# Dilated attention with upper and lower heads issued in turn, gates behind the attention, the memory's key slabs at the end

## The chip, the cores and the metric

The kernel runs on one core of a Trainium2 chip. The metric is the device time of one execution in microseconds (us). The engines are TensorE (PE; its weight loads are listed as PEld), VectorE (DVE), ScalarE (ACT), GpSimd (POOL) and SyncE (SP), which issues the large DMAs. Each engine works through its own list of instructions in a fixed order. An instruction whose input is late holds up everything behind it on its engine.

## The reference

A stream of 256 tokens with 1024 features goes through two blocks of layers. Only one part is touched here, the mixer of the second block and the memory attention that follows it:

```python
h = rmsnorm_2(x, mix_norm[l])
z = h @ w_in[l]                       # 2 x 512 for the gate, 3 x 512 for q, k, v
z_sgu = jax.nn.gelu(z[..., :2 * D_SGU], approximate=False)
...
y_a = chunked_spatial_gating(z_sgu, sgu_ln_g[l], sgu_ln_b[l], sgu_w_s[l], sgu_b_s[l])
y_b = dilated_mixture_attention(q, k, v).reshape(b, s, D_ATT)
y = jnp.concatenate([rmsnorm_2(y_a, out_norm_a[l]), rmsnorm_2(y_b, out_norm_b[l])], axis=-1)
x = x + y @ w_out[l]
h = rmsnorm_2(x, cross_norm[l])
m = rmsnorm_2(mem, mem_norm[l])
x = x + memory_cross_attention(h, m, cross_wq[l], cross_wk[l], cross_wv[l], cross_wo[l])
```

The dilated attention has 8 heads of 64 features. The kernel computes it as one softmax attention whose mask carries the logarithm of how many of the three dilated patterns contain a key. The gate normalises one half of `z_sgu` in groups of 64, mixes it along the tokens with a causal 128x128 matrix per group, and multiplies the result with the other half.

## The kernel before, in words

The activation `x` stays on the chip with features on the partitions. Weights come in slabs of 1 MB. SP loads a slab into one of two `raw` buffers (line 277), ACT rounds each half to `whi` (line 293), DVE computes the rest `wlo` (line 295). Five half slabs can be alive at once, and a slab is prepared two slabs ahead of its use (`W_AHEAD = 2`). A `raw` buffer is free again when the second `wlo` of its slab is done. A product with a slab is three matmuls per tile (lines 320 to 322).

Matmul results go to PSUM. There are eight banks: two called `mm`, two `tr`, four `acc`. Each name is a ring: a new tile takes the bank of the oldest tile of that name, once that one has been read.

The order of the mixer's work is written out in the string `MIX`. Its words:

- `v`, `w`, `x`, `y` are products of the normed tokens with two slabs of `w_in` each. `v` feeds the gate's values (`gate_values`: gelu, group norm over several DVE passes, one pow on POOL). `w` and `x` give q and k, `y` gives the attention's values.
- `r0`, `r1` turn q and k by their positions and transpose them, for the first and the second 128 tokens.
- `u0`, `u1` are the other half of the gate (one slab each, gelu in `gates`).
- `00`, `01` and `10` to `13` are steps of the attention, for the first and the second 128 tokens.
- `g0`, `g1` are the gate's mixing matmuls (`gating`, line 1357) with the multiplication and the norm behind them (`normed`).
- `N` loads and norms the memory (into a `raw` buffer). `K0` to `K3` are its four slabs of keys.

Behind the string stands the output product `w_out`.

A step of the attention before handles 4 heads (first tokens) or 2 heads (second tokens, with twice the keys). All heads of a step lie in the same half of the partitions. The step adds the mask by two matmuls with the identity (line 587), computes the scores (line 591, 64 of 128 rows of the array), the softmax on DVE and ACT (lines 594 to 612), transposes the probabilities (line 401), copies them (line 619), and multiplies with the values (line 625, 64 of 128 columns). The instructions' final order on each engine is set by a scheduler that moves instructions of later words ahead where their inputs allow, as far as the rings of buffers let it.

Of the kernel before, what the change touches and what calls it, by code (L numbers as in the profile page):

```python
# [12 lines left out]
AF = mybir.ActivationFunctionType  # L13
ALU = mybir.AluOpType
AX = mybir.AxisListType

P = 128
# [7 lines left out]
SCALE = 0.125  # L25
# [21 lines left out]

EVEN = "p0 i0 N x1 W0 t0 p1 i1 h0 W1 h1 i2 m0 m1 00 x0 10 i3 W2 s0 W3 11 12 01 x2 m2 g0 13 g1 g2 m3 x3 g3"

MIX = "x N v w y r0 r1 u0 10 u1 00 K0 11 g0 01 12 g1 13 K1 K2 K3"  # L50


def weight_plan():
# [14 lines left out]
    def ffn(kind, layer):  # L68
        for c in range(11):
            feat(f"{kind}_gate", layer, c * 256, 256)  # L70
            feat(f"{kind}_up", layer, c * 256, 256)
        for c in range(11):
            plan.append((f"{kind}_down", layer, "d", c * 16, 0))
# [29 lines left out]
    ffn("ffn1", 0)  # L103
    for f in MIX.split():
        if f[0] in "vwxy":
# [132 lines left out]
class Kernel:  # L238
# [331 lines left out]
    def attention(self, pool, t, qt, kt, kblock, v, vcol, bias, nsink):  # L570

        nc = self.nc
        nk = t + 1
        per = 4 // nk
        keys = nk * P
        den = self.small([P, 8], "den")
        mneg = self.small([P, 8], "mneg")
        mx = self.small([P, 8], "mx")  # L580
        po = self.ps("acc")

        def step(g):
            sc = self.ps("mm")
            scv = sc.rearrange("p (h k) -> p h k", h=per)
            for m, bt in enumerate(bias):
                nc.tensor.matmul(sc, self.ident_r, bt, start=(m == 0), stop=False)
            for i in range(per):
                half, qb = divmod(g * per + i, 4)
                r = slice(half * 64, half * 64 + 64)  # L590
                nc.tensor.matmul(scv[:, i, :], qt[r, qb, t * P:(t + 1) * P],  # L591
                                 kt[r, kblock(qb), 0:keys], start=False, stop=(i == per - 1))
            hs = slice(g * per, (g + 1) * per)
            nc.vector.tensor_reduce(mx[:, hs], scv, axis=AX.X, op=ALU.max)
            if nsink is None:
                nc.vector.tensor_scalar(mneg[:, hs], mx[:, hs], -SCALE, None, ALU.mult)
            else:
                nc.vector.scalar_tensor_tensor(mneg[:, hs], mx[:, hs], -SCALE, nsink[:, hs],
                                               ALU.mult, ALU.min)
                es = self.small([P, per], f"es{per}")  # L600
                nc.vector.tensor_tensor(es, mneg[:, hs], nsink[:, hs], ALU.subtract)
            pr = self.t(pool, [P, per, keys], "prob", bufs=4)
            for i in range(per):
                h = g * per + i
                nc.scalar.activation(pr[:, i, :], scv[:, i, :], AF.Exp, bias=mneg[:, h:h + 1],
                                     scale=SCALE, accum_out=den[:, h:h + 1])
            if nsink is not None:
                nc.scalar.activation(es, es, AF.Exp)
                nc.vector.tensor_tensor(den[:, hs], den[:, hs], es, ALU.add)
            nc.vector.reciprocal(den[:, hs], den[:, hs])  # L610
            e = nc.gpsimd if nsink is not None and NORMP[t] == "g" else nc.vector
            e.tensor_tensor(pr, pr, den[:, hs].unsqueeze(2).to_broadcast([P, per, keys]), ALU.mult)
            tp = self.ps("tr")
            for i in range(per):
                for b in range(nk):
                    c = i * nk + b
                    self.transpose(tp[:, c * P:(c + 1) * P], pr[:, i, b * P:(b + 1) * P])
            pt = self.t(pool, [P, 4, P], "prob", bufs=4)
            nc.scalar.copy(pt, tp.rearrange("p (c n) -> p c n", c=4))
            for i in range(per):  # L620
                half, qb = divmod(g * per + i, 4)
                r = slice(half * 64, half * 64 + 64)
                h = 2 * qb + half
                for b in range(nk):
                    nc.tensor.matmul(po[r, qb * P:(qb + 1) * P], v[b][:, vcol(h):vcol(h) + 64],  # L625
                                     pt[:, i * nk + b, :], start=(b == 0), stop=(b == nk - 1))

        return [lambda g=g: step(g) for g in range(8 // per)], po.rearrange("p (b n) -> p b n", b=4)


    def setup(self):
# [632 lines left out]
    def mix(self):  # L1264
        nc, a = self.nc, self.a
        stack = ExitStack()
        mp = self.pool("mix", stack=stack)
# [34 lines left out]
        vt = [self.t(mp, [P, 512], f"vt{t}") for t in range(NT)]  # L1302
        qt, kt = self.t(mp, [P, 4, 256], "qt"), self.t(mp, [P, 4, 256], "kt")
        oa, ob = self.operand(), self.operand()

        def normed(y, gain, op, t):

            sq = self.t(self.wk, [P, 512], "sq", bufs=2)
            nc.scalar.activation(sq.rearrange("p (b n) -> p b n", b=4), y, AF.Square)
            nc.gpsimd.tensor_tensor(sq[:, :256], sq[:, :256], sq[:, 256:], ALU.add)  # L1310
            r, _ = self.inv_rms([sq[:, b * P:(b + 1) * P] for b in range(2)], 512, 1e-6, "rn")
            yn = self.t(mp, [P, 4, P], "yn", bufs=2)
            for b in range(4):
                nc.vector.scalar_tensor_tensor(yn[:, b, :], y[:, b, :], self.prm[:, gain + b:gain + b + 1],
                                               r, ALU.mult, ALU.mult)
            s = slice(t * P, (t + 1) * P)
            self.split_ps(yn, op[0][:, :, s], op[1][:, :, s])

        def dilated(t):
            v = qk[:, t].rearrange("p i (h d) -> p (i h) d", d=64)  # L1320
            x1, x2 = v[:, :, 0:8], v[:, :, 8:16]
            c = self.cos[:, t, :].unsqueeze(1).to_broadcast([P, 16, 8])
            s = self.sin[:, t, :].unsqueeze(1).to_broadcast([P, 16, 8])
            t1, t2, t3, t4 = (self.t(mp, [P, 16, 8], f"ro{i}", bufs=2) for i in range(4))
            nc.vector.tensor_tensor(t1, x1, c, ALU.mult)
            nc.vector.tensor_tensor(t2, x2, s, ALU.mult)
            nc.vector.tensor_tensor(t3, x2, c, ALU.mult)
            nc.vector.tensor_tensor(t4, x1, s, ALU.mult)
            nc.vector.tensor_tensor(x1, t1, t2, ALU.subtract)
            nc.vector.tensor_tensor(x2, t3, t4, ALU.add)  # L1330
            for i, dst in enumerate((qt, kt)):
                ps = self.ps("tr")
                for b in range(4):
                    self.transpose(ps[:, b * P:(b + 1) * P], qk[:, t, i, b * P:(b + 1) * P])
                d = dst[:, :, t * P:(t + 1) * P]
                if i == 0:
                    nc.scalar.copy(d, ps.rearrange("p (b n) -> p b n", b=4))
                else:
                    nc.vector.tensor_copy(d, ps.rearrange("p (b n) -> p b n", b=4))
            if t == 0:  # L1340
                bias = [x[:, 128:].unsqueeze(1).to_broadcast([P, 4, P]) for x in (dh, dl)]
            else:
                bias = [x.unsqueeze(1).to_broadcast([P, 2, 256]) for x in (dh, dl)]
            return self.attention(mp, t, qt, kt, lambda b: b, vt, lambda h: h * 64, bias, None)

        su = self.t(mp, [P, 4, 256], "su")

# [3 lines left out]
            nc.scalar.activation(d, d, AF.Gelu)  # L1351

        def gating(t):
            ps = self.ps("acc")
            for g in range(8):
                r = slice((g % 2) * 64, (g % 2) * 64 + 64)
                nc.tensor.matmul(ps[r, (g // 2) * P:(g // 2 + 1) * P], sv[t][:, g * 64:(g + 1) * 64],
                                 ws[:, g, :], start=True, stop=True)
            ya = self.t(mp, [P, 4, P], "ya", bufs=2)
            nc.vector.tensor_tensor(ya, ps.rearrange("p (b n) -> p b n", b=4), bst, ALU.add)  # L1360
            nc.vector.tensor_tensor(ya, ya, su[:, :, t * P:(t + 1) * P], ALU.mult)
            normed(ya, PR_ONA, oa, t)
# [3 lines left out]
        def step(t, i):  # L1366
            att[t][0][i]()
            if i + 1 == len(att[t][0]):
                normed(att[t][1], PR_ONB, ob, t)

        for f in MIX.split():
            c = int(f[1:] or 0)
            if f == "v":
                self.gemm_tok(ops, "w_in", 0, 512, gate_values)
            elif f in "wxy":
                i = "wxy".index(f)
# [182 lines left out]
```

## Time and profile before

| what | us |
|---|---|
| median of 3 runs (1245.34 to 1247.02) | 1246.55 |
| the profiled execution | 1243.83 |
| its span | 1242.1 |
| PE busy | 1211.7 |
| DVE busy | 868.8 |
| ACT busy | 676.6 |
| POOL busy | 211.2 |

The span is the stretch between the first and the last recorded instruction. A busy PE is not a PE at its peak: matmuls overlap, and 64-row or 64-column matmuls use half of the array. The mixer lies at about 850 to 980 us of the span; its attention at 903 to 953 us. What the kernel can win or lose there is read from the time that PE spends on its attention's matmuls and from the time it waits between them.

### The profile page before, as it was taken

To read this page: it belongs to the slowest core of one execution; us is meant where nothing else is said; L and a number is where in the kernel's file an instruction comes from. 1 tells how busy PE (TensorE), PEld (TensorE's weight loads), DVE (VectorE), ACT (ScalarE), POOL (GpSimd) and SP (SyncE) were. 2 spreads that over 40 slices of the span, in tenths; PEclk is the share of its full clock that TensorE was granted. 3 is DMA by queue.
4 is the path that set the end of the run, shared out by engine and by line. 5 is a ranking of instruction groups with operands and counts; after the bars stand their busy time and mean duration, and the time that the engine had idled before them with its cause. 6 is when DMAs were issued, how large, how long until landed. Compare 5 with 4: busy or idle time off the path is not lost.

```text
span 1242.1 us, 19044 instructions
## 1 busy us (share of the span) xinstructions
PE 1211.7 (98%) x7686; PEld 1072.7 (86%) x7686; DVE 868.8 (70%) x1191; ACT 676.6 (54%) x1052; POOL 211.2 (17%) x177
## 2 busy tenths in 40 slices
PE   6889999999999999999999999999999999999997
PEld 6777998888899879888888888888889999888886
DVE  8978588777665647877766867766866656777752
ACT  6543566565446755655545655545664545655542
POOL 7665021110010002101001110002201101111000
PEclk9978999999999999999999999999999999999998
DMA  6541355555553325455654545646633434555551
GB/s 208 172 158 53 139 172 194 180 201 203 180 197 110 131 68 204 170 187 186 216 191 174 196 177 198 204 174 212 209 131 103 155 118 139 190 183 201 204 200 38
DMA packets 36776, 208.86 MB, mean 168 GB/s; under 512 B 3920, under 2 KB 9808, under 8 KB 12752
## 3 DMA queue, kind: packets, MB, share of 16 engines
q1 hardware_dynamic: 35824, 205.48, 47.7%
q0 software_dynamic: 576, 1.64, 0.5%
q8 instruction: 60, 0.98, 0.3%
q10 hardware_dynamic: 288, 0.52, 0.1%
q14 instruction: 28, 0.23, 0.1%
HBM read 205.57 MB, written 2.06 MB: 167 GB/s over the span
## 4 chain that ended last, share of the span: by engine, by line
PE 92%; DVE 5%; DMA 1%; issue 1%; ACT 1%; POOL 0%; DVEq 0%; ACTq 0%
PE acc L367 26%; PE acc L366 13%; PE mm L367 13%; PE mm L366 7%; PE mm L320 4%; PE mm L322 4%; PE mm L321 4%; PE acc L322 4%; PE acc L321 4%; PE acc L320 4%; PE mm L591 1%; PE tr L401 1%; PE acc L1191 1%; DVE wlo L295 1%; PE acc L625 1%; DVE a L454 1%
## 5 line engine op out<-in xcount | busy, mean ns | idle before, releaser
L295 DVE TENSOR_TENSOR wlo<-raw,whi 128x1024 fp32r<-128x1024 f32 (+1 forms) x378 | 472.0, 1251 | 225.1 <-ACT whi L293 223.6
L293 ACT CAST whi<-raw 128x1024 fp32r<-128x1024 f32 (+1 forms) x378 | 392.4, 1043 | 280.8 <-DMA raw<-in_wts 111.2
L367 PE MATMUL acc<-h,whi 128*128 128x512 f32 x704 | 247.8, 397 | 0.0
L367 PE MATMUL mm<-a,whi 128*128 128x512 f32 x704 | 247.0, 392 | 0.0
L367 PE MATMUL acc<-a,whi 128*128 128x512 f32 x704 | 246.0, 392 | 0.0
L366 PE MATMUL acc<-h,wlo 128*128 128x256 f32 x704 | 196.9, 281 | 0.0
L366 PE MATMUL mm<-a,wlo 128*128 128x256 f32 x704 | 196.6, 281 | 0.0
L366 PE MATMUL acc<-a,wlo 128*128 128x256 f32 x704 | 196.3, 280 | 0.0
L367 PEld LDWEIGHTS acc<-h,whi 128*128 128x128 f32 x704 | 131.9, 188 | 32.0
L367 PEld LDWEIGHTS mm<-a,whi 128*128 128x128 f32 x704 | 131.5, 187 | 28.5
L367 PEld LDWEIGHTS acc<-a,whi 128*128 128x128 f32 x704 | 130.9, 187 | 28.2
L366 PEld LDWEIGHTS acc<-a,wlo 128*128 128x128 f32 x704 | 133.0, 189 | 1.0
L366 PEld LDWEIGHTS acc<-h,wlo 128*128 128x128 f32 x704 | 132.9, 189 | 0.3
L366 PEld LDWEIGHTS mm<-a,wlo 128*128 128x128 f32 x704 | 132.6, 189 | 0.2
L546 POOL TENSOR_TENSOR sg<-sg,rb 128x512 f32<-128x512 f32 x44 | 58.2, 1326 | 388.8 <-ACT sg L545 379.2
L463 POOL TENSOR_TENSOR ssq<-ssq,sq 128x512 f32<-128x512 f32 x26 | 39.7, 1528 | 416.7 <-ACT sq L461 253.2
L320 PE MATMUL mm<-a,whi 128*128 128x256 f32 x224 | 66.4, 298 | 6.7 <-ACT whi L293 6.7
L321 PE MATMUL acc<-a,whi 128*128 128x256 f32 x240 | 67.4, 284 | 0.0
L322 PE MATMUL acc<-a,wlo 128*128 128x256 f32 x240 | 67.1, 285 | 0.0
L322 PE MATMUL mm<-a,wlo 128*128 128x256 f32 x224 | 66.1, 296 | 0.8 <-DVE wlo L295 0.7
L320 PE MATMUL acc<-a,whi 128*128 128x256 f32 x240 | 66.0, 286 | 0.0
L321 PE MATMUL mm<-a,whi 128*128 128x256 f32 x224 | 65.8, 295 | 0.0
(371 smaller groups left out, 1951.5 us busy)
## 6 DMA issues: line engine op xcount, KB each, us to landing
raw<-in_wts SPq DMA_DIRECT2D x187, 1024.0 KB, 4.9
raw<-in_mem SPq DMA_DIRECT2D x4, 512.0 KB, 5.6
eb<-lag SPq DMA_DIRECT2D x4, 512.0 KB, 4.8
x<-in_x SPq DMA_DIRECT2D x4, 256.0 KB, 5.3
raw<-in_wts SPq DMA_DIRECT2D x4, 256.0 KB, 5.6
sprm<-in_prm SPq DMA_DIRECT2D x1, 512.0 KB, 9.1
ud<-s SPq DMA_DIRECT2D x1, 512.0 KB, 2.6
uu<-ud SPq DMA_DIRECT2D x8, 64.0 KB, 5.3
```

Source lines behind the costliest of these rows:

```text
L293: nc.scalar.copy(hi[:, c:c + n], src)
L295: nc.vector.tensor_tensor(lo[:, c:c + n], src, hi[:, c:c + n].bitcast(F32), ALU.subtract)
L320: mm(out, a[0], b[0], start=start, stop=False, skip_group_check=True)
L321: mm(out, a[0], b[1], start=False, stop=False, skip_group_check=True)
L322: mm(out, a[1], b[0], start=False, stop=stop, skip_group_check=True)
L366: mm(out[:, 0, :], w[1], x[:, 0], start=first, stop=False, skip_group_check=True)
L367: mm(out, w[0], x, start=False, stop=last, skip_group_check=True)
L401: self.nc.tensor.transpose(out, in_, self.ident[:k, :k])
L454: lo = nc.vector.scalar_tensor_tensor(lo, x[:, b, :], g, hi.bitcast(F32), ALU.mult, ALU.subtract).ins
L463: nc.gpsimd.tensor_tensor(ssq, ssq, q, ALU.add)
L546: nc.gpsimd.tensor_tensor(sg, sg, rb2, ALU.mult)
L591: nc.tensor.matmul(scv[:, i, :], qt[r, qb, t * P:(t + 1) * P], kt[r, kblock(qb), 0:keys], start=False, stop=(i == per - 1))
```

## The change

A new function, `attention_pairs`, takes the place of `attention` in the mixer. One of its steps handles heads of both halves of the partitions: 8 heads for the first tokens (one step, `00`), 4 heads for the second (two steps, `10` and `11`). Scores of the lower and of the upper half follow each other in turn, each into a bank of its own, and so do the products with the values. Masks, transposes, softmax instructions and copies keep their number. The scores now take two `acc` banks per step instead of one `mm` bank, and the gate's mixing takes an `mm` bank instead of an `acc` bank. The probabilities of a step have one transposed buffer (`probt`) instead of a share in a ring of four.

The order string puts the memory's norm `N` between `u0` and `u1`, the value product `v` behind the first attention steps, both gates behind the last one, and all four key slabs at the end.

```diff
-MIX = "x N v w y r0 r1 u0 10 u1 00 K0 11 g0 01 12 g1 13 K1 K2 K3"
+MIX = "x w y r0 r1 10 00 v 11 u0 N u1 g0 g1 K0 K1 K2 K3"
...
+    def attention_pairs(self, pool, t, qt, kt, v, bias):
+        nc = self.nc
+        nk = t + 1
+        per = 4 // nk
+        keys = nk * P
...
+        po = self.ps("acc")
+
+        def softmax(half, g, scv, pt):
+            hs = slice(half * 4 + g * per, half * 4 + (g + 1) * per)
+            nc.vector.tensor_reduce(mx[:, hs], scv, axis=AX.X, op=ALU.max)
+            nc.vector.tensor_scalar(mneg[:, hs], mx[:, hs], -SCALE, None, ALU.mult)
+            pr = self.t(pool, [P, per, keys], "prob", bufs=2)
+            for i in range(per):
+                h = hs.start + i
+                nc.scalar.activation(pr[:, i, :], scv[:, i, :], AF.Exp, bias=mneg[:, h:h + 1],
+                                     scale=SCALE, accum_out=den[:, h:h + 1])
+            nc.vector.reciprocal(den[:, hs], den[:, hs])
+            nc.vector.tensor_tensor(pr, pr, den[:, hs].unsqueeze(2).to_broadcast([P, per, keys]), ALU.mult)
+            tp = self.ps("tr")
...
+            nc.scalar.copy(pt, tp.rearrange("p (c n) -> p c n", c=4))
+
+        def step(g):
+            scs = [self.ps("acc") for _ in range(2)]
...
+            for i in range(per):
+                qb = g * per + i
+                for half in range(2):
+                    r = slice(half * 64, half * 64 + 64)
+                    nc.tensor.matmul(scv[half][:, i, :], qt[r, qb, t * P:(t + 1) * P],
+                                     kt[r, qb, 0:keys], start=False, stop=(i == per - 1))
+            pt = self.t(pool, [P, 2, 4, P], "probt")
+            for half in range(2):
+                softmax(half, g, scv[half], pt[:, half])
+            for i in range(per):
+                qb = g * per + i
+                for b in range(nk):
+                    for half in range(2):
+                        r = slice(half * 64, half * 64 + 64)
+                        c = (2 * qb + half) * 64
+                        nc.tensor.matmul(po[r, qb * P:(qb + 1) * P], v[b][:, c:c + 64],
+                                         pt[:, half, i * nk + b, :], start=(b == 0), stop=(b == nk - 1))
...
-            return self.attention(mp, t, qt, kt, lambda b: b, vt, lambda h: h * 64, bias, None)
+            return self.attention_pairs(mp, t, qt, kt, vt, bias)
...
         def gating(t):
-            ps = self.ps("acc")
+            ps = self.ps("mm")
```

New line numbers of the changed kernel, as the orders below have them: masks 667, scores 672, maximum 646, negative 647, exponential 651, reciprocal 653, division 654, copy 660, values 683, gate mixing 1415, `su` 1408.

PE of the kernel before, where the transposed probabilities of step `00` and the scores of `12` and `01` stand (`mm_8860` is the key slab `K0`):

```order
L320 MATMUL mm_8860<-m_1450_8341,whi_8683 128x256
L321 MATMUL mm_8860<-m_1450_8341,whi_8683 128x256
L401 MATMUL tr_8838<-ident_80,prob_8831 128x128 x4
L322 MATMUL mm_8860<-m_1450_8341,wlo_8684 128x256
L587 MATMUL mm_8910<-dilh_8196,identr_82 128x512
L587 MATMUL mm_8910<-dill_8198,identr_82 128x512
L591 MATMUL mm_8910<-kt_8261,qt_8260 128x256 x2
L587 MATMUL mm_8966<-dilh_8196,identr_82 128x512
L587 MATMUL mm_8966<-dill_8198,identr_82 128x512
L591 MATMUL mm_8966<-kt_8261,qt_8260 128x128 x4
```

The whole key slab `K0` (48 matmuls) lies there between a step's scores and the transposes of its probabilities.

PE of the changed kernel, from the last scores of `00` (banks `acc_8578`, `acc_8579`) through those of `11` (`acc_8752`, `acc_8753`):

```order
L672 MATMUL acc_8579<-kt_8261,qt_8260 128x128
L401 MATMUL tr_8602<-ident_80,prob_8595 128x128 x4
L401 MATMUL tr_8617<-ident_80,prob_8610 128x128 x4
L683 MATMUL acc_8506<-probt_8592,vt_1429_8258 64x128
L667 MATMUL acc_8752<-dilh_8196,identr_82 128x512
L667 MATMUL acc_8752<-dill_8198,identr_82 128x512
L667 MATMUL acc_8753<-dilh_8196,identr_82 128x512
L667 MATMUL acc_8753<-dill_8198,identr_82 128x512
L672 MATMUL acc_8752<-kt_8261,qt_8260 128x256
L672 MATMUL acc_8753<-kt_8261,qt_8260 128x256
L672 MATMUL acc_8752<-kt_8261,qt_8260 128x256
L672 MATMUL acc_8753<-kt_8261,qt_8260 128x256
```

No slab lies between the scores of `00` and the transposes of their own probabilities any more, and `v`, `u0` and `u1` are all done ahead of this place.

PE of the changed kernel a little later, from the transposes of `11` to the first matmul of `K0` (`mm_9061`); `mm_8984` and `mm_9017` are the two gates:

```order
L401 MATMUL tr_8770<-ident_80,prob_8765 128x128 x4
L401 MATMUL tr_8783<-ident_80,prob_8778 128x128 x4
L683 MATMUL acc_8532<-probt_8762,vt_1429_8258 64x128
L429 MATMUL tr_8634<-diag_8640,ones_73 128x128
L683 MATMUL acc_8532<-probt_8762,vt_1429_8258 64x128
L683 MATMUL acc_8532<-probt_8762,vt_1430_8259 64x128 x2
L683 MATMUL acc_8532<-probt_8762,vt_1429_8258 64x128 x2
L683 MATMUL acc_8532<-probt_8762,vt_1430_8259 64x128 x2
L1415 MATMUL mm_8984<-ws_8207,sv_1426_8255 64x128 x8
L1415 MATMUL mm_9017<-ws_8207,sv_1427_8256 64x128 x8
L419 MATMUL tr_8800<-ones_73,sq_8797 128x1 x2
L320 MATMUL mm_9061<-m_1552_8882,whi_8820 128x256
```

`K0` moved from between the attention's steps to behind both gates, whose banks it takes over.

DVE of the changed kernel ahead of the softmax of `00` (`m` is the memory's operand, `wlo_8825` belongs to `K0`, `wlo_8926` and `wlo_8930` to `K1`):

```order
L1408 TENSOR_TENSOR su_8264<-mm_8828,rb_8253 128x512
L454 SCALAR_TENSOR_TENSOR m_1552_8882<-raw_8879,prm_77,m_1552_8882 128x256
L295 TENSOR_TENSOR wlo_8825<-raw_8818,whi_8824 128x1024
L454 SCALAR_TENSOR_TENSOR m_1553_8883<-raw_8879,prm_77,m_1553_8883 128x256 x4
L1408 TENSOR_TENSOR su_8264<-mm_8933,rb_8253 128x512
L295 TENSOR_TENSOR wlo_8926<-raw_8923,whi_8925 128x1024
L295 TENSOR_TENSOR wlo_8930<-raw_8923,whi_8929 128x1024
L646 TENSOR_REDUCE mx_8505<-acc_8578 128x4
L646 TENSOR_REDUCE mx_8505<-acc_8579 128x4
L647 TENSOR_SCALAR mneg_8504<-mx_8505 128x4 x2
```

Both `wlo` of `K1` stand ahead of the maximum of `00`, and behind the memory's operand, which moved here from the mixer's beginning.

## Rows read from the trace of the kernel before

**Rows 1.** The page's busy times: us, share of the span, instructions.
```profile
PE 1211.7 (98%) x7686; PEld 1072.7 (86%) x7686; DVE 868.8 (70%) x1191; ACT 676.6 (54%) x1052; POOL 211.2 (17%) x177
```

**Rows 2.** Waits of PE, 860 to 980: us in total, times, longest.
```profile
PE acc L625 <- ACT prob L619: 1.1, 2, 0.7
PE mm L587 <- ACT prob L605: 0.3, 1, 0.3
```

**Rows 3.** Timeline of PE in the attention: start, us, engine, line, operation, records.
```profile
903.78 1.13 PE L591 MATMUL mm<-kt,qt 64*128 64x256 f32 x4
904.84 0.39 PE L320 MATMUL mm<-a,whi 128*128 128x256 f32 x1
...
910.68 0.40 PE L587 MATMUL mm<-dilh,identr 128*128 128x512 f32 x1
910.91 0.40 PE L587 MATMUL mm<-dill,identr 128*128 128x512 f32 x1
...
916.16 1.09 PE L625 MATMUL acc<-prob,vt 128*64 128x128 f32 x8
...
924.83 1.96 PE L1357 MATMUL acc<-ws,sv 128*64 128x128 f32 x29
```

**Rows 4.** Timeline of DVE in the attention.
```profile
906.47 0.68 DVE L594 TENSOR_REDUCE mx<-mm 128x2 f32<-128x512 f32 x1
907.18 0.17 DVE L596 TENSOR_SCALAR mneg<-mx 128x2 f32<-128x2 f32 x1
...
909.98 0.69 DVE L612 TENSOR_TENSOR prob<-prob,den 128x512 f32<-128x512 f32 x1
910.72 1.22 DVE L295 TENSOR_TENSOR wlo<-raw,whi 128x1024 fp32r<-128x1024 f32 x1
...
933.71 1.14 DVE L1314 SCALAR_TENSOR_TENSOR yn<-ya,prm,rn 128x128 f32<-128x128 f32 x4 [1.23 <-ACT rn L431]
```

**Rows 5.** Timeline of ACT in the attention.
```profile
907.43 1.28 ACT L605 ACT_TABLE_LOAD   x1 [1.60 <-DVE mneg L596]
908.73 0.47 ACT L605 ACTIVATE prob<-mm,mneg 128x256 f32<-128x256 f32 x1
...
909.64 2.21 ACT L293 CAST whi<-raw 128x1024 fp32r<-128x1024 f32 x2
...
913.70 0.57 ACT L619 COPY prob<-tr 128x512 f32<-128x512 f32 x1
...
915.85 0.37 ACT L605 ACTIVATE prob<-mm,mneg 128x128 f32<-128x128 f32 x1
...
917.24 1.06 ACT L293 CAST whi<-raw 128x1024 fp32r<-128x1024 f32 x1
```

**Rows 6.** Instructions of line 408: count, ns least/median/most, first and last start.
```profile
L408 POOL TENSOR_TENSOR rln<-rln,nhalf x2: 2489/2531/2573, 880.8 to 885.6; 128x8 f32<-128x8 f32 x2
```

**Rows 7.** The page's DMA issues: count, KB each, us to landing.
```profile
raw<-in_wts SPq DMA_DIRECT2D x187, 1024.0 KB, 4.9
raw<-in_mem SPq DMA_DIRECT2D x4, 512.0 KB, 5.6
```

**Rows 8.** Instructions on the memory's operand m: ns least/median/most, starts.
```profile
L453 ACT ACTIVATE m<-raw,prm x8: 492/496/509, 861.5 to 867.4; 128x256 fp32r<-128x256 f32 x8
L454 DVE SCALAR_TENSOR_TENSOR m<-raw,prm,m x8: 471/484/1529, 862.1 to 869.2; 128x256 fp32r<-128x256 f32 x8
```

**Rows 9.** Windows: us, busy of PE, PEld, DVE, ACT, POOL; granted clock, DMA share, GB/s.
```profile
60.00:64.00 4.00, 1.19 (x5) 1.20 (x6) 4.00 (x6) 0.00 (x0) 1.73 (x2) 0.59 0.01 2
68.00:72.00 4.00, 4.00 (x36) 4.00 (x37) 1.56 (x5) 2.01 (x4) 3.02 (x3) 1.00 0.96 369
84.00:88.00 4.00, 3.99 (x20) 3.41 (x18) 1.90 (x4) 0.94 (x2) 4.00 (x5) 0.57 0.48 145
100.00:104.00 4.00, 4.00 (x20) 2.75 (x18) 2.96 (x5) 0.38 (x1) 3.77 (x4) 0.79 0.00 0
932.00:936.00 4.00, 3.27 (x18) 1.99 (x17) 2.38 (x7) 1.59 (x6) 0.00 (x0) 1.00 0.02 4
```

More of the change, by code (lines that the diff above doesn't have):

```diff
@@ L628, in attention @@
         return [lambda g=g: step(g) for g in range(8 // per)], po.rearrange("p (b n) -> p b n", b=4)
+    def attention_pairs(self, pool, t, qt, kt, v, bias):
[3 more added lines that the diff above has]
+        keys = nk * P
+        den = self.small([P, 8], "den")
+        mneg = self.small([P, 8], "mneg")
+        mx = self.small([P, 8], "mx")
+        po = self.ps("acc")
[13 more added lines that the diff above has]
+                for b in range(nk):
+                    c = i * nk + b
+                    self.transpose(tp[:, c * P:(c + 1) * P], pr[:, i, b * P:(b + 1) * P])
+            nc.scalar.copy(pt, tp.rearrange("p (c n) -> p c n", c=4))
+        def step(g):
+            scs = [self.ps("acc") for _ in range(2)]
+            scv = [sc.rearrange("p (h k) -> p h k", h=per) for sc in scs]
+            for sc in scs:
+                for m, bt in enumerate(bias):
+                    nc.tensor.matmul(sc, self.ident_r, bt, start=(m == 0), stop=False)
+            for i in range(per):
[7 more added lines that the diff above has]
+                softmax(half, g, scv[half], pt[:, half])
+            for i in range(per):
+                qb = g * per + i
+                for b in range(nk):
+                    for half in range(2):
[3 more added lines that the diff above has]
+                                         pt[:, half, i * nk + b, :], start=(b == 0), stop=(b == nk - 1))
+        return [lambda g=g: step(g) for g in range(4 // per)], po.rearrange("p (b n) -> p b n", b=4)
```

## The prediction

> **What bounds the kernel now.** I read the busy times first, then who waited for whom on PE in the mixer, then the timelines of PE, DVE and ACT there, and the granted clock last. PE is busy for 98% of the span [rows 1], and in the mixer it waits for 1.1 + 0.3 = 1.4 us in all [rows 2]. So the kernel is bound by PE's list. An edit helps only by what it takes out of that list, and it hurts by each wait that it puts in. The softmax of a step is long, but before it is covered, since PE has a slab to multiply meanwhile.
>
> **What the pairing takes out.** Unpaired, two score matmuls of 256 keys last about 1.06 (903.78 to 904.84, four records), and eight records of the value product about 1.02 [rows 3]. The mixer has six steps, each with one such group of either kind: 6.4 and 6.1 us. The gate's matmuls have the value product's shape, but take their column halves in turn: 29 records in 1.96 less the last one's tail of 0.2, or 0.06 each, against 0.13 [rows 3]. So halves in turn run side by side for columns, and the value product should halve: -3.1 us. For row halves in turn this trace has no row. Bounds: nothing, or another -3.2. I take -3.2, as the column row is the nearest.
> The Trainium skill (TensorEngine Tiling, Key Properties) says of row and column tiles alike that different tiles load and multiply in parallel; the columns in this trace agree (0.06 against 0.13), the rows are not shown. By that rule the scores halve too.
>
> **What the new order puts in.** Before, the slab `K0` separates scores from transposes. After, PE has done `v`, `u0` and `u1`, and then comes a list without any slab: values of `10`, scores of `00`, its transposes, scores of `11`, its values, both gates, and only then `K0`, which must take the gates' `mm` bank. PE has to sit out two softmaxes and the gate's DVE passes. I count from the end of `v`, t = 0.
>
> *PE reaches the list.* `u0` and `u1` last 5.84 each (904.84 to 910.68 [rows 3]); with eight transposes PE is through at 12.6.
>
> *DVE reaches the softmax of `00`.* DVE must first finish the memory's operand and `wlo` of `K1`. The memory's load waits for `u1`'s last `wlo`, about t = 0.4, and lands 5.6 later [rows 7], at 6.0. On ACT follow four copies at 0.5 [rows 8], a square at about 0.6 and the cast of `K0`'s second half at 1.06 [rows 5]: 9.6. Its `wlo` takes 1.2 [rows 4]: 10.8. That frees the `raw` buffer for `K1`, which lands 4.9 later [rows 7], at 15.7; two casts and a `wlo` make it 19.0. The operand's DVE part was up to 1.53 each; I take the median 0.48 [rows 8], as POOL has nothing to do in this stretch. The scores themselves are ready at about 16.3, so DVE is the later one: S = 19.0.
>
> *From S to `K0`.* All from rows 3 to 5 unless named:
> - two maxima at 0.6, a negative 0.17: 1.4. Exponential table 1.28, as gelu ran before: 2.7. Eight exponentials, four in 1.39 (915.85 to 917.24): 5.5. The cast queued behind them and two copies: 7.5.
> - Masks of `11`, four at 0.33 (910.91 to 911.24 by the rhythm of its rows): 8.8; paired scores 0.55: 9.4; values 0.5: 9.9.
> - On ACT two squares (the norm's, the gate's) stand ahead of the exponentials of `11`: 11.0. Four exponentials at 0.46 (908.73 to 909.64): 12.9. The second gate half's square: 13.5.
> - DVE: the division and the gate's sum of squares, 0.6 to 0.7 each (as every 128x512 pass): 14.5.
> - POOL scales and raises to a power; the latter alone takes 2.53 [rows 6], and a short norm step stands between: 18.2.
> - DVE: the gate's scaling 0.6, four `yn` passes 1.14, two more gate passes 1.2: 21.1; the gate's evacuation, behind one more pass, frees the bank: 22.4.
>
> So `K0` starts at 19.0 + 22.4 = 41.4, and PE spends 28.8 us from 12.6 on a list that holds some 10 us of work.
>
> *`K2`.* It takes `K0`'s bank, whose scaled copy needs the memory's norm. That norm's squares now come behind the attention on ACT, and its last matmul stands behind `K1`. From there a cast 1.06, a small copy 0.3, a `wlo` 1.2 and the copy 0.69 make 3.0; PE has 0.9 of small matmuls meanwhile: 2.1 of wait.
>
> **The clock.** In 60 to 64 PE was busy for 1.19 of 4 us and the granted clock fell to 0.59; in 68 to 72, after dense matmuls, it is back at 1.00. After the gaps before 84 it was 0.57 and came back only in 100 to 104 [rows 9]. With 3.27 busy of 4 it stayed at 1.00 (932 to 936). In the new list PE waits for 8 us in one piece (16.3 to 24.5), so I expect the lower level, 1.2 GHz, from there on. Masks, scores, transposes and values in the chain then cost another 2.9 us, and about 5.5 us of `K0` run at half speed, as in 62 to 68, which loses 2.7.
>
> **The sum.** The same work before: scores 6.4, values 6.1, twelve masks at 0.33 = 4.0, gates 2.1, 24 transposes of about 0.12 = 3.0, small norm matmuls 0.8, waits 1.4: 23.8 us. After: the list 28.8 + 2.9, step `10` inside `v` and `u1` 2.7 (masks 1.2, scores 0.5, transposes 1.0), `K2`'s wait 2.1, the slow start 2.7: 39.2. The difference is +15.4. The `x`, `w`, `y`, `v`, `u` and `K` slabs and the output product cost the same on PE, and their splits on ACT and DVE stay hidden behind it, as they did before, when PE waited for no split in the mixer [rows 2]; if that cover went, each half slab would cost PE up to its `wlo` of 1.2. The profiled execution took 1243.8, so I expect one of about 1259.2. It lies 2.7 under the median of the runs shown; on the median's scale that is 1262.
>
> ScalarE: Activation LUTs (What ACT_TABLE_LOAD costs) in the Trainium skill gives a switch of tables a drain of 1.38 us besides a load of 1.28. Here the load took 1.28 and the next exponential began at once (907.43, 908.73 [rows 5]), so the trace knows no drain behind it. By the page the chain would have one more in front of `00`: 1263.4 on the median's scale, an estimate.
>
> **The rivals.**
> - *The clock stays up.* For it: 3.27 of 4 busy did not lower it. Against it: the gap here is much longer. Without the 2.9 and the 2.7 the change costs +9.8: 1256.3.
> - *The clock stays down long, or the rows don't pair.* The stretch 84 to 100 shows half speed for 16 us in attention work. 16 us of slow slabs lose 8.0 instead of 2.7, so 5.3 more; if the scores don't run side by side, which would be the change not doing what it says, about 2.5 more come on top (0.5 in each step, twice that at the lower clock). +20.7 to +23.2: 1267.3 to 1269.8.
> - *Faster: the waits are hidden.* If the softmaxes were back before PE needs them, the pairing's 6.3 and the old waits of 1.4 would be won: 1238.8. It holds as long as PE's wait between `u1` and `K0` stays below about 8 us. For it: before, PE waits for only 1.4 us on the same softmaxes. Against it: there a slab of 5.8 us lay between, and PE's list now has nothing there. Two softmaxes alone take about 5 us each from scores to transposes.
> - *No change* would need a wait of 6 to 10 us: DVE free at 16, no gate chain behind. The pow alone speaks against it.
>
> **How the numbers follow.** The forecast has 0.55, the clock that stays up 0.23, the long slow clock or unpaired rows 0.16, hidden waits 0.04, no change 0.02. About 0.2% (2.5 us) is what a measurement of this kernel can tell from no change. So slower has 0.94, within 0.2% 0.02, faster 0.04. The range for 8 in 10 goes from 1250 (clock up, and the loads of the memory and of `K1` land early, which takes some 3 us off S, with small chains shorter by as much) to 1275 (the slow clock to the end, rows unpaired, and the sum of some 25 hand-overs between engines short by a few us).
>
> **What would show it.** Right: the largest waits of PE in the mixer are transposes of the probabilities for the division, the value product for the copy, the gate's matmuls for `sv`, and `K2` for `kt`; the granted clock falls between `u1` and `K1`; DVE starts the maxima of `00` behind `wlo` of `K1`. Value records come at about 0.06. Wrong: PE busy without a gap of 3 us between `u1` and `K0`, or a `K0` that starts within 18 us of `u1`'s end.

## The result: 1256.9 us, slower by 0.9%

| | before | after |
|---|---|---|
| median, us | 1246.57 (1245.34 to 1247.02) | 1256.93 (1256.27 to 1257.45) |
| the profiled execution, its span | 1243.83, 1242.1 | 1256.27, 1254.6 |
| mean granted clock | 0.986 | 0.975 |
| from the first matmul of `x` to the first of `w_out` | 108.9 | 121.0 |

The ratio is 1.0089 with a 95% interval of 1.0073 to 1.0105, so 9 to 13 us. The forecast was 1262.0, a difference of +15.4; the median gives +10.4 and the profiled executions +12.4. The mixer alone explains it: before, `x` starts at 849.80 and `w_out` at 958.70; after, the two stand at 850.10 and 971.10, which is 12.1 us more.

The page's busy line of the kernel after, beside [rows 1]:

```profile
PE 1215.6 (97%) x7686; PEld 1077.2 (86%) x7686; DVE 870.8 (69%) x1191; ACT 678.6 (54%) x1052; POOL 208.1 (17%) x177
```

PE is busy for 3.9 us longer on the same 7686 matmuls, but that is not the mixer's loss: 3.8 of it lie ahead of `x` (828.95 before, 832.76 after), where the clock was low for longer in this execution. From `x` to `w_out` PE is busy for 107.5 us in both. Two things cancel there. Two kinds of matmuls got shorter, and a matmul at half clock (granted clock 0.50, 1.2 of 2.4 GHz) is booked as longer work: four transposes take 1.08 at 922.39 and 0.63 at 932.98, at full clock. What is left of the loss are the waits of PE in the mixer, 13.4 us where there were 1.4 [rows 2] (us in total, times, longest):

```profile
PE tr L401 <- ACT prob L651: 7.0, 1, 7.0
PE tr L419 <- POOL sq L1368: 1.6, 1, 1.6
PE mm L1415 <- DVE sv L1357: 1.2, 1, 1.2
PE tr L401 <- DVE rs L423: 1.0, 1, 1.0
PE mm L320 <- DVE kt L482: 0.9, 1, 0.9
PE tr L419 <- ACT mrb L431: 0.7, 1, 0.7
...
```

The timeline of PE, beside [rows 3] (start, us, then what; in brackets the idle time ahead):

```profile
911.53 0.43 PE L683 MATMUL acc<-probt,vt 128*64 128x128 f32 x2
...
912.55 1.09 PE L683 MATMUL acc<-probt,vt 128*64 128x128 f32 x14
...
914.24 1.16 PE L672 MATMUL acc<-kt,qt 64*128 64x128 f32 x16
922.39 1.08 PE L401 MATMUL tr<-ident,prob 128*128 128x128 f32 x4 [7.00 <-ACT prob L651]
923.79 1.09 PE L401 MATMUL tr<-ident,prob 128*128 128x128 f32 x4 [0.31 <-DVE prob L654]
...
927.43 1.40 PE L672 MATMUL acc<-kt,qt 64*128 64x256 f32 x8
...
932.98 0.63 PE L401 MATMUL tr<-ident,prob 128*128 128x128 f32 x4 [0.96 <-DVE rs L423]
...
940.39 1.09 PE L1415 MATMUL mm<-ws,sv 128*64 128x128 f32 x16 [1.24 <-DVE sv L1357]
...
957.78 0.38 PE L320 MATMUL mm<-m,whi 128*128 128x256 f32 x1 [0.92 <-DVE kt L482]
```

Scores of 128 keys in the kernel before:

```profile
922.87 1.16 PE L591 MATMUL mm<-kt,qt 64*128 64x128 f32 x8
```

Values come 14 records in 1.09 where [rows 3] has 8 in 1.09, and scores of 128 keys 16 records in 1.16 where there were 8. So both kinds run side by side. Then PE has nothing to do from 915.4 to 922.39. `K0` starts at 942.05.

The DVE timeline of the same place and one row of ACT, beside [rows 4, 5]:

```profile
914.77 2.36 DVE L295 TENSOR_TENSOR wlo<-raw,whi 128x1024 fp32r<-128x1024 f32 x2 [2.45 <-ACT whi L293]
917.05 1.28 DVE L646 TENSOR_REDUCE mx<-acc 128x4 f32<-128x512 f32 x2
...
921.34 0.18 DVE L653 RECIPROCAL den<-den 128x4 f32<-128x4 f32 x1 [2.80 <-ACT prob L651]
```

```profile
918.51 1.28 ACT L651 ACT_TABLE_LOAD   x1 [2.82 <-DVE mneg L647]
```

The maxima of `00` stand behind both `wlo` of `K1`, as the order says, and start 1.65 us after the scores are done (917.05 and 915.40).

Windows of 4 us, with the columns of [rows 9]:

```profile
912.00:916.00 4.00, 3.40 (x34) 2.30 (x34) 1.55 (x3) 2.62 (x3) 0.00 (x0) 1.00 0.24 100
916.00:920.00 4.00, 0.00 (x0) 0.00 (x0) 2.54 (x5) 1.48 (x2) 0.00 (x0) 0.72 0.42 131
...
924.00:928.00 4.00, 4.00 (x12) 2.44 (x13) 0.90 (x1) 0.71 (x2) 0.00 (x0) 0.50 0.02 4
928.00:932.00 4.00, 2.44 (x26) 1.75 (x22) 2.24 (x6) 2.12 (x7) 0.92 (x2) 1.00 0.00 0
...
936.00:940.00 4.00, 3.15 (x32) 2.69 (x30) 3.15 (x8) 1.22 (x3) 1.25 (x1) 0.72 0.00 0
...
960.00:964.00 4.00, 4.00 (x27) 4.00 (x27) 1.49 (x3) 1.07 (x2) 0.08 (x1) 0.73 0.01 4
```

The clock falls in the gap, is back at 1.00 in 928 to 932 after PE was busy for all of 924 to 928, and is below full again in 932 to 940 (0.85 and 0.72) and in `K2` (956 to 964, 0.84 and 0.73).

### The profile page after: what moved, and what is told of

It is laid out like the page before. It is cut to its first block, busy times and chain, and to the rows that moved or that the text cites. A ratio compares the mean times of both kernels' runs of the same rounds, so it can differ in the third digit from the quotient of the medians.

```text
span 1254.6 us, 19043 instructions
## 1 busy us (share of the span) xinstructions
PE 1215.6 (97%) x7686; PEld 1077.2 (86%) x7686; DVE 870.8 (69%) x1191; ACT 678.6 (54%) x1052; POOL 208.1 (17%) x177
## 4 chain that ended last, share of the span: by engine, by line
PE 90%; DVE 5%; ACT 2%; issue 1%; DMA 1%; POOL 0%; DVEq 0%; ACTq 0%
PE acc L367 26%; PE acc L366 13%; PE mm L367 13%; PE mm L366 7%; PE acc L322 4%; PE acc L320 4%; PE acc L321 4%; PE mm L320 4%; PE mm L321 4%; PE mm L322 4%; PE tr L401 1%; DVE wlo L295 1%; PE acc L1249 1%; PE tr L419 1%; DVE a L454 1%
```

## The experiments

All ran beside the kernel before. Theory A: the order costs, because softmaxes, gates and norms have no slab beside them, and the pairing itself gains. Theory B: the pairing or the new banks cost. Theory C, later: one paired step at a time is too long a chain whatever lies beside it. "x to w_out" is read from the profile as above, "waits" are PE's in the mixer. The ratios are those on record and not quotients of the medians. "Rest" is what is left over the paired work at full clock, 101.4 us (the pairs with `N` first: 104.1 less 2.7 of waits, every stretch at clock 1.00), or over the unpaired work of before, 108.9 - 1.4 = 107.5. Most of it is half clock: the mean granted clock from `x` to `w_out` was 0.93 in the changed kernel, against 1.00 before. That half clock is all of it isn't shown.

| kernel | median | ratio to before, 95% | x to w_out | waits | rest |
|---|---|---|---|---|---|
| after | 1256.9 | 1.0089 [1.0073, 1.0105] | 121.0 | 13.4 | 6.2 |
| pairs between slabs | 1252.9 | 1.0044 [1.0022, 1.0067] | 114.6 | 10.1 | 3.1 |
| old steps, new order | 1264.8 | 1.0135 [1.0091, 1.0179] | 124.7 | 9.3 | 7.9 |
| `N` ahead of `r0` | 1262.7 | 1.0120 [1.0079, 1.0160] | 125.6 | 15.7 | 8.5 |
| `K0` ahead of gates | 1258.1 | 1.0080 [1.0055, 1.0105] | 120.0 | 11.6 | 7.0 |
| gates in `acc` | 1260.8 | 1.0109 [1.0078, 1.0140] | 123.4 | 11.1 | 10.9 |
| pairs covered | 1249.7 | 1.0022 [1.0004, 1.0040] | 114.4 | 8.0 | 5.0 |
| the same, unpaired | 1249.5 | 1.0029 [1.0009, 1.0049] | 113.9 | 5.2 | |
| gap filled | 1255.3 | 1.0066 [1.0045, 1.0088] | 120.2 | 8.6 | |
| pairs, `N` first | 1242.8 | 0.9979 [0.9963, 0.9995] | 104.1 | 2.7 | 0 |
| the same, unpaired | 1245.7 | 0.9993 [0.9980, 1.0006] | 109.9 | 3.0 | |
| `N` ahead of `w` | 1255.4 | 1.0067 [1.0049, 1.0085] | 121.8 | 12.2 | 8.2 |
| old steps, `N` first | 1256.7 | 1.0080 [1.0057, 1.0103] | 117.7 | 7.6 | 2.6 |

**Pairs between slabs.**

```diff
-MIX = "x w y r0 r1 10 00 v 11 u0 N u1 g0 g1 K0 K1 K2 K3"
+MIX = "x N v w y r0 r1 u0 10 u1 00 K0 11 g0 K1 g1 K2 K3"
```

> The paired attention and the bank swap of the change stay; only the order string is written as in the kernel before (x N v w y r0 r1 u0 10 u1 00 K0 11 g0 K1 g1 K2 K3), so that a slab lies between the scores of each step and its transposes. Theory A (the loss is the order: softmaxes and the gate's chain with no slab beside them): PE waits in the mixer fall from 13.4 us to at most 3, what is left is the pairing's gain of about 6.3 us on PE, so 1240 (1237 to 1244), faster than the kernel before. Theory B (the pairing itself or the swap of acc and mm banks costs the time): the loss stays, 1250 or more, with waits at the bank rings or at the one transposed buffer per step.

By its time it is on theory B's side (1250 or more), by its waits on neither: one of 1.5 is for an `mm` bank, the others are not for banks. The loss is halved, and up to the end of `K3` (849.21 to 953.06, 103.9 us) PE has no wait between scores and transposes. But step `11` now ends with the last slab, and its norm and the gates' stand bare ahead of `w_out`:

```profile
953.06 1.29 PE L419 MATMUL tr<-ones,sq 128*128 128x1 f32 x8 [0.71 <-POOL sq L1368]
...
960.77 0.80 PE L429 MATMUL tr<-diag,ones 128*128 128x128 f32 x2 [2.65 <-DVE diag L426]
...
963.80 1.22 PE L320 MATMUL acc<-a,whi 128*128 128x256 f32 x4 [2.23 <-ACT a L396]
```

From 953.06 to 963.80 the 10.7 us are norms. The clock falls with them (0.61 in 960 to 970), and from the first matmul of `w_out` to the end it takes 285.3 us instead of 283.4. Neither theory had this wait, and it takes back the pairing's gain.

**Old steps in the new order.** The kernel before, with

```diff
-MIX = "x N v w y r0 r1 u0 10 u1 00 K0 11 g0 01 12 g1 13 K1 K2 K3"
+MIX = "x w y r0 r1 10 11 00 01 v 12 13 u0 N u1 g0 g1 K0 K1 K2 K3"
```

> The kernel before with its own unpaired attention and its own banks, and the order string of the change, each paired step written as its two unpaired ones (10 11 00 01 v 12 13 u0 N u1 g0 g1 K0 K1 K2 K3). The order that comes out is not the change's word for word: the scores need the two mm banks, so some slabs stay between the later steps, and the first four steps follow each other without one. Theory A (the order is what costs): PE waits some 8 us there (two softmaxes of about 3 to 4 us to get a bank back), 1254 (1250 to 1260). Theory B (the pairing or the bank swap costs): no loss without it, 1246.6 within 2.

1264.8, more than theory A gave and far from B's 1246.6. Without any pairing this order loses 15.8 us between `x` and `w_out`, so a loss needs neither the pairing nor the new banks. It is not the same loss, though: 5.2 us of the waits here are for the two `mm` banks that the unpaired scores need. What decides against B comes below, with `N` first.

**N ahead of r0**, from the changed kernel:

```diff
+MIX = "x w y N r0 r1 10 00 v 11 u0 u1 g0 g1 K0 K1 K2 K3"
```

> The changed kernel with one word moved: the memory's load and norm N stand behind y again, ahead of the attention, not between u0 and u1. Theory A in its detail (the maxima of step 00 stand on DVE behind the memory's operand and behind wlo of K1, and K2 waits for the memory's norm): the maxima start when the scores land, about 1.7 us earlier, and K2's wait of 1.65 and the half clock behind it (about 1.5) go; 1252 (1250 to 1254). Rival: the delay of the softmax is only the lack of a slab, DVE is not late because of the memory: 1257 within 1.5.

A miss for theory and rival alike, slower instead of faster. The maxima of `00` do follow their scores at once, but `r0`, `r1` came late, the scores of `10` only at the end of `u1`, and so three softmaxes stand without a slab (waits of 4.4 and 4.1 at the transposes of `10` and `00`).

**K0 ahead of the gates**, from the changed kernel:

```diff
+MIX = "x w y r0 r1 10 00 v 11 u0 N u1 K0 g0 g1 K1 K2 K3"
```

> The changed kernel with one word moved: K0 stands ahead of the two gates, which puts its 48 matmuls between the scores of step 00 and their transposes. Theory A: the wait of 7.0 us at those transposes is filled by the slab of 5.8 us, and the clock need not fall there; the second gate now takes the first one's bank (about 1.5 more); 1251 (1248 to 1253). Theory B: no wait is what costs, so the move changes nothing, 1257 within 1.5.

The wait at the transposes of `00` shrank from 7.0 to 1.2, yet only 1.0 us of it came out from `x` to `w_out`, and nothing in the median, which lies where theory B had it. The chain from the maxima of `00` to the first gate starts and ends as in the changed kernel, and then the second gate waits:

```profile
923.92 0.63 PE L401 MATMUL tr<-ident,prob 128*128 128x128 f32 x4 [1.17 <-ACT prob L651]
...
933.42 0.63 PE L401 MATMUL tr<-ident,prob 128*128 128x128 f32 x4 [0.96 <-DVE prob L654]
...
945.15 1.78 PE L1415 MATMUL mm<-ws,sv 128*64 128x128 f32 x16 [2.96 <-DVE rs L423]
```

It takes the first gate's bank, as expected, but that one had been read by 942.26. What came last are its own values: the DVE pass at line 1357 ended at 945.01. It took 1.75 us, and the passes at lines 1356 and 397 before it 1.23 and 1.15, where such a pass takes 0.68 elsewhere; POOL ran its additions at that time (lines 1368 and 463, 940.39 to 944.45). `K1` then begins at clock 0.50 (948 to 952). The slab went ahead of the chain's end, and the gain was given back behind it. That the chain sets the end is the better reading, not that waits cost nothing.

**Gates in an acc bank**, from the changed kernel:

```diff
         def gating(t):
-            ps = self.ps("mm")
+            ps = self.ps("acc")
```

> The changed kernel with one word changed: the gates' mixing takes an acc bank again (the banks of the last scores, which are free by then), not an mm bank. The order string stays, but K0 and the first half of K1 now stand between the scores of step 00 and their transposes, since no gate holds their banks. Theory A (PE's list without slabs costs, and the mm banks of the gates are what pushes K0 behind them): 8.9 us of slab lie beside the softmax of 00, which then comes about 2 us later, and the norms behind the gates stand without cover ahead of K2 (some 4 us): 1251 (1247 to 1254). Rival (as the kernel with K0 ahead of the gates showed: the chain from the maxima of 00 to the last gate sets the end whatever lies beside it, and what is gained in front is given back behind): 1255 or more.

The rival's side, and beyond it. Nearly two slabs moved ahead, and the gates and four norms were left in one bare stretch, at half clock throughout:

```profile
936.00:940.00 4.00, 2.84 (x12) 2.25 (x12) 3.49 (x10) 2.19 (x4) 3.58 (x4) 0.50 0.58 238
...
952.00:956.00 4.00, 1.86 (x8) 1.78 (x8) 2.61 (x8) 1.33 (x3) 1.61 (x4) 0.50 0.00 0
...
960.00:964.00 4.00, 4.00 (x21) 4.00 (x21) 1.49 (x6) 0.62 (x1) 0.56 (x1) 0.50 0.02 4
```

**The gap filled**, added to the changed kernel behind the scores of a step:

```diff
+            if t == 0:
+                spare = self.ps("tr")
+                for n in range(26):
+                    nc.tensor.matmul(spare, self.ident_r, bias[0], start=(n == 0), stop=(n == 25))
```

> The changed kernel with 26 spare matmuls (128x512, into a spare tr bank, their result unused) on PE between the scores of step 00 and their transposes, about 6 us of the 7.0 us that PE waits there. The output is unchanged. Theory of the forecast (the half clock behind the wait costs 2.9 us in the list from 00 to the gates): the clock stays at 1.00 there and the time falls to 1254. Rival (work at half clock lies beside the softmax on DVE and ACT, which sets the pace): 1256.5 within 1. If the spare matmuls delay the transposes: up to 1258.

Undecided between the two (1.0066 and 1.0089 have intervals that overlap), and the premise failed. The clock stayed up for one stretch and then fell all the same:

```profile
920.00:924.00 4.00, 2.92 (x15) 1.97 (x13) 1.25 (x4) 3.99 (x18) 0.00 (x0) 1.00 0.54 225
924.00:928.00 4.00, 3.37 (x12) 2.06 (x14) 1.71 (x2) 1.55 (x3) 0.00 (x0) 0.64 0.00 0
```

So the clock falls without the one long gap too. Counted from `x`, the transposes of `00` come at 72.4 (72.3 in the changed kernel) and `K0` at 92.7 (92.0). Filling the gap moved nothing on the chain.

**Pairs covered, and the same unpaired.**

```diff
+MIX = "x w v r0 r1 y 10 u0 00 u1 N g0 g1 11 K0 K1 K2 K3"
```

The unpaired one also has in `step`, for scores and value products alike:

```diff
-            for i in range(per):
-                qb = g * per + i
-                for half in range(2):
+            for half in range(2):
+                for i in range(per):
+                    qb = g * per + i
```

> The paired attention with an order string of its own: x w v r0 r1 y 10 u0 00 u1 N g0 g1 11 K0 K1 K2 K3. The gate's values come first, a slab stands beside each of the three softmaxes, both gates come ahead of the last step, and two slabs and the output product stand behind it, so that no norm is waited for at the end. Theory A (only the uncovered waits cost; what is left of the change is the pairing's gain): the stretch from x to the output product is 103 to 107 us where the kernel before has 108.9, 1242 (1239 to 1245), faster than the kernel before. Theory C (one paired step at a time, with two score banks and one transposed buffer, makes the chain of three softmaxes longer than the slabs beside it): 1247 or more.

> The same order string and steps as the one with pairs covered, but scores and value products run through one half of the partitions first and then through the other, so that halves are not in turn. Theory A (both kinds pair: 3.2 us for rows, 3.1 us for columns, in a stretch where PE is the bound): 5 to 6.5 us more than the paired one. Rival (only columns run side by side): 3 us more. Rival (the time of that stretch is the softmax chain's, not PE's): no difference.

No step waits for its softmax any more, but the time stayed above before's. What is late now are norms: one of the mixer's, waited for 3.1 us, and the memory's, 3.5 us in two waits (2.8 and the rest of the 3.7), which holds `K0`'s bank and so `K2`:

```profile
PE tr L429 <- DVE diag L426: 3.7, 2, 3.1
PE tr L419 <- POOL ssq L471: 2.8, 1, 2.8
```

From 940 to 952 the clock is 0.50. This looked like theory C until `N` was moved. Unpairing changed nothing here (third case of its expectation), since PE waits for the same norms.

**Pairs with N first, and the same unpaired.**

```diff
+MIX = "x N w v r0 r1 y 10 u0 00 u1 g0 g1 11 K0 K1 K2 K3"
```

> The paired attention with the order string x N w v r0 r1 y 10 u0 00 u1 g0 g1 11 K0 K1 K2 K3: as in the kernel with pairs covered, but with the memory's load and norm ahead of w, so that K2 does not wait for the memory's norm (there that wait and the half clock behind it cost some 10 us). A slab or the gates stand beside each softmax, two slabs beside each norm. Theory A (only uncovered waits cost; the rest of the change is the pairing's gain): from x to the output product 101 to 104.5 us where the kernel before has 108.9, and 1240 (1238 to 1243), faster than the kernel before. Theory C (one paired step at a time is too long a chain whatever lies beside it): 1246 or more.

> The same order string, the halves of the partitions one after the other and not in turn (scores and value products). Theory A (both kinds pair, and here PE is the bound): 5 to 6.3 us more than the paired one. Rival (PE waits for the softmax chain in this stretch too): within 1 us of it.

The paired kernel is faster than the kernel before by a little, 0.9979 (0.9963 to 0.9995), and C falls. B falls with it: the pairing and the new banks are those of the changed kernel, and the order string alone takes the time from 1256.9 to 1242.8. It has 2.7 us of waits left, and 104.1 us from `x` to `w_out`, inside theory A's bounds. Its waits:

```profile
PE mm L320 <- ACT sv L1346: 1.2, 1, 1.2
PE tr L401 <- ACT prob L651: 1.0, 1, 1.0
PE tr L401 <- ACT whi L293: 0.5, 1, 0.5
```

The unpaired one is slower by 2.9 us by the medians, between theory A and its rival, with intervals that overlap, so the times don't separate the two kernels. The traces do in the mixer: 109.9 us from `x` to `w_out` against 104.1. Two things make less of these 5.8. Behind the first matmul of `w_out` the paired kernel takes 285.9 us to the end, the unpaired one 283.7 and the kernel before 283.4, so 2.2 to 2.5 us of its gain are lost there again; no run shows why. And the unpaired order still pairs in part (busy us and mean ns of one, 880 to 975; the paired kernel first):

```profile
L683 PE MATMUL acc<-probt,vt 128*64 128x128 f32 x48 | 4.6, 282 | 0.0
...
L672 PE MATMUL acc<-kt,qt 64*128 64x256 f32 x16 | 2.3, 402 | 0.0
...
L672 PE MATMUL acc<-kt,qt 64*128 64x128 f32 x16 | 1.2, 285 | 0.0
```

```profile
L683 PE MATMUL acc<-probt,vt 128*64 128x128 f32 x48 | 6.7, 280 | 0.0
...
L672 PE MATMUL acc<-kt,qt 64*128 64x256 f32 x16 | 3.0, 408 | 0.0
...
L672 PE MATMUL acc<-kt,qt 64*128 64x128 f32 x16 | 2.1, 291 | 0.0
```

These are 8.1 against 11.8 us; the kernel before has 6.5 + 4.8 + 2.6 = 13.9 in the same groups. Scores of the two halves that only follow each other already run side by side in part.

**N ahead of w**, from the changed kernel:

```diff
+MIX = "x N w y r0 r1 10 00 v 11 u0 u1 g0 g1 K0 K1 K2 K3"
```

> The changed kernel with one word moved: N stands ahead of w (x N w y r0 r1 10 00 v 11 u0 u1 g0 g1 K0 K1 K2 K3), not ahead of r0 as in the kernel with N early, which held up r0, r1 and step 10 and so left a third softmax without a slab. Step 10 lies inside v again. Theory A (the memory's operand holds up DVE ahead of the maxima of 00, and its norm holds up K2): the maxima of 00 follow the scores at once (1.65 us gained), 11 matmuls of u1 stand behind the scores (1.3), K2 does not wait (1.65) and runs at full clock (1.5): from x to the output product 115 (121.0 in the changed kernel), 1251 (1249 to 1253). Rival (the memory has no part in the loss): 1257 within 1.5.

Mostly a miss: 1255.4, near the rival. The detail is right (maxima at 918.40, scores done at 918.36; `K2` does not wait), but ACT takes it back:

```profile
919.84 1.04 ACT L293 CAST whi<-raw 128x1024 fp32r<-128x1024 f32 x1 [4.53 <-PE mm L321]
920.90 1.28 ACT L651 ACT_TABLE_LOAD   x1
...
925.11 1.28 ACT L1409 ACT_TABLE_LOAD   x1
...
933.29 1.28 ACT L651 ACT_TABLE_LOAD   x1 [5.30 <-DVE mneg L647]
```

A cast stands ahead of the exponentials of `00`, and the gelu of `u1` now lies between those of `00` and `11`, so that the table is loaded twice more. The clock is mostly at 0.50 from 924 to 944, and from the transposes of `00` to `K0` it takes 23.8 us instead of 19.7.

**Old steps with N first**, from the kernel before:

```diff
+MIX = "x N w v r0 r1 y 10 11 u0 00 01 u1 g0 g1 12 13 K0 K1 K2 K3"
```

> The kernel before with its own unpaired attention and banks and the order of the kernel with pairs and N first, each paired step written as its two unpaired ones (x N w v r0 r1 y 10 11 u0 00 01 u1 g0 g1 12 13 K0 K1 K2 K3). It tells what that order is worth without the pairing. Theory A: no gain without the pairing, 1246.5 (1244 to 1250, more if the scores' two mm banks make PE wait). Rival (the order and not the pairing is what gains): as fast as the paired kernel of the same order.

1256.7, slower than before: two unpaired steps in a row hold both `mm` banks, and slabs wait 5.0 us for them. The gain needs the paired steps together with their `acc` banks, which no run separates; this order without them loses.

## Why the prediction was right

The direction, the place and the mechanism hold; the time was 5.1 us too high and within the range. That it came so near is in part luck, since errors of both signs cancel. By its steps, with t = 0 at 899.06, where `v` ends and `u0` begins:

- *Pairing, -6.3.* Sound. Between the kernel before and the pairs with `N` first, the work between `x` and `w_out` without waits fell from 107.5 to 101.4, by 6.1 (5.8 by the rows of its matmuls, 13.9 and 8.1). The row halves, taken by the column row because before had none, pair.
- *PE at the list at 12.6.* The list begins at 911.53: 12.5.
- *S = 19.0.* It was 18.0. ACT began with the memory at 904.01, 1.0 earlier than forecast; the chain over both `wlo` of `K1` is the one predicted.
- *S to `K0`, 22.4 + 2.9 = 25.3.* 917.05 to 942.05 is 25.0, but its two terms were not right. The 2.9 are for half clock in masks, scores, transposes and values, and the clock was back at 1.00 from 928 on, before most of the values. With `K0` ahead of the gates it was 1.00 in all of 920 to 932, and from the first transposes of `00` to those of `11` PE took 9.5 us (923.92 to 933.42), against 10.6 in the changed kernel (922.39 to 932.98). That puts the half clock at some 1.1 us up to there, an estimate, since casts and copies lie a little otherwise in that run. So the 22.4 were too low by about as much as the 2.9 were too high. The pow was shorter than forecast (1.65 and 2.17, not 2.53), and `K0` came 0.5 after the end of the gate's evacuation (941.54). `K0` started at t = 43.0 (forecast 44.3 with the half clock).
- *Which waits.* The transposes for the softmax (7.0), the gate for `sv` (1.2) and `K2` (0.7 + 0.9 = 1.65, forecast 2.1, where the four terms of the forecast add up to 3.25 and not 3.0) are there. The value product did not wait for its copy; that wait shows at the next transposes instead (0.7).
- *The clock.* The step that was mis-sized. It fell where expected, but `K0` ran at full speed (its 48 matmuls come at 0.12 each), so the 2.7 of a slow start is zero. Behind its own wait, `K2` then lost some 1.6, which was not forecast (42 matmuls in 6.63 us from 957.78; at 0.12 each, 5.04).

Together: -1.0 for S, -0.3 for the chain, +0.1 for PE, which was at the list earlier, -2.7 for `K0`, -0.5 for `K2`'s wait and +1.6 for its half clock make -2.8, and 15.4 - 2.8 = 12.6 against 12.4 in the profiled executions. The rival with the clock up (1256.3) is nearer to the median by number, but not in kind: the clock was down, at other places. On the trace's own scale the 121.0 us are 101.4 of work, 13.4 of waits and 6.2 mostly of half clock.

ScalarE: Activation LUTs (What ACT_TABLE_LOAD costs) in the Trainium skill would put 1.38 us of drain beside the load. Here as well the load at 918.51 took 1.28 and the first exponential began at 919.80, so the trace has no drain behind it. TensorEngine Tiling (Array Packing), Key Properties, in the Trainium skill says that different tiles can multiply in parallel. The trace agrees for row tiles too, with sixteen score records in 1.16.

What stays open: what the second low stretch of the clock (932 to 940) costs by itself, since no run held the clock up there and left the rest as it was.

## What to carry to other kernels

Pairing row and column halves is worth its 6 us of PE, but only where PE is what is waited for; in the best order here some 3 us of it came out in the whole time. Before merging steps, count the slabs that stand beside each softmax, each gate and each norm to the end of the stage: a slab moved ahead of one wait is taken from another, and each bare wait can also cost the clock behind it. Look at the last norm before the next big product, and at which bank the late one holds.

## What was not expected of the hardware

- Row halves that follow each other in the list (two score matmuls of the lower half, then two of the upper) took as long as halves in turn. It holds for this step, where nothing stands between the halves. The unpaired kernel with `N` first, and then the paired one:

```profile
899.74 1.14 PE L672 MATMUL acc<-kt,qt 64*128 64x256 f32 x8
```

```profile
901.37 1.14 PE L672 MATMUL acc<-kt,qt 64*128 64x256 f32 x8
```

- DVE passes beside additions on POOL often took much longer. In the kernel after, the multiplication at line 1419 took 1.74 and 1.06 us beside POOL's line 463; with `K0` ahead of the gates it took 0.68 at 945.00, when that addition was over. The diagonal at line 426 took 1.38 where it took 0.29 at 934.86 without such an addition. It is not so for every pass: line 1418, which reads one input from PSUM, took 0.68 beside POOL's line 1368, and there it was POOL that took longer (1.29, at 930.63 alone 0.73). These runs don't show the cause.
- The granted clock of the kernel after was 1.00 in 928 to 932, with PE busy for 2.44 of 4 us there and for all 4 just before. With gates in `acc` it stayed at 0.50 in 956 to 960, where PE was busy for 3.34, and in 960 to 964, where PE was busy throughout; it was 0.89 in the next 4 us.
